# A second pair of blocks by seven products, a constant written later, and other banks for the second layer's first group

## The chip, the cores and the metric

The kernel runs on one core of one Trainium2 chip. The metric is device time in microseconds of one execution. Times in the trace are microseconds from the start of the profiled span unless marked ns.

The engines are named as the profile names them: PE is TensorE's matrix product and PEld its weight load, DVE is VectorE, ACT is ScalarE, POOL is GpSimd, SP is SyncE. A "product" below is one matmul instruction.

## The reference

A two-layer encoder over 512 tokens of width 1024. Each layer has a mixer of three gated attentions and then a feed-forward part with a convolution:

```python
def conv_ffn(h, w_up, conv_w, conv_b, w_down):
    u = h @ w_up                                  # 512 x 1024 by 1024 x 5632
    u = depthwise_conv_width_3(u, conv_w) + conv_b
    a, g = jnp.split(u, 2, axis=-1)               # 2816 each: "value" and "gate" half
    return (jax.nn.gelu(g) * a) @ w_down

for l in range(2):
    h = rmsnorm(x, norm1_g[l])
    x = x + gated_parallel_mixer(h, ...)          # three attentions, merged by gates, @ w_out
    h = rmsnorm(x, norm2_g[l])
    x = x + conv_ffn(h, ...)
return rmsnorm(x, final_g)
```

All data are float32. The up projection's 5632 columns are 44 blocks of 128: blocks 0 to 21 of the value half (p = 0) and 0 to 21 of the gate half (p = 1).

## The kernel before, in words

**Precision.** A float32 operand is split into a high part and the rest (`hi`, `lo`, both in the type fp32r), and each product of two operands is done as three: hi by hi, hi by lo, lo by hi (`mm3`, lines 222 to 224). Activations lie transposed, 128 features by 512 tokens, as eight tiles `hh`, `hl`; weights are the stationary side.

**A plain block.** `dense` multiplies one block of 128 output columns: 8 tiles of the inner dimension x 3 products, each 128 x 128 by 128 x 512, into one bank of PSUM (`ps_d`). Then `conv` (lines 1105 ff.) reads the bank: ScalarE writes `c` (L1113), VectorE adds the two neighbours (L1115, L1116). In a gate block ScalarE applies the GELU (L1120), VectorE multiplies with the value block kept in `ca` (L215 `prod`), and `operands` makes what the down projection reads: high and low parts of the product and of sums of its quarters (L1139 to L1155).

**Seven products.** Where two neighbouring blocks, pairs of inner tiles and the two halves of the tokens form a 2 x 2 x 2 product, the kernel uses seven half-size products instead of eight (a Strassen-like scheme). The down projection and part of the output projection do so for all columns (`do_sum`, L1175 to L1177). `do_us` does it for one pair of blocks of the up projection in each layer, chosen by `UPS = ((9, 1),)`: pair 9 of the gate half, blocks 18 and 19. A unit is 7 steps x 4 pairs of inner tiles x 3 products of 128 x 128 by 128 x 256 (L1066 to L1068), in four banks. It needs
- sums of weights: `load_sum` loads four quarters of the weight block (one of them twice) on SP's queue and adds two of them by adding DMAs from GpSimd's queue (lines 173, 174); VectorE makes two more sums (L189, L192);
- sums of the activations: `whole` copies `hh` to `hx` and adds `hl` by DMA, `mix` makes the sums and splits them (`hs`). This is done once a layer, after block 12, four times `mix` after four later blocks;
- evictions: partial results go to `u1`, `u2` by ScalarE (L1071 to L1081) and VectorE (L1075, L1079, L1084), and `conv` reads `u1`, `u2` instead of a bank.

**Order.** TensorE's and SP's instructions run in the order that `schedule` writes out by hand: value block and gate block in turn, `("up", f)`, the unit `("us", 9, 1)` in the place of its second block, then `cover`, `rest` and the sums of the down projection. VectorE's, ScalarE's and GpSimd's order in this part comes from a planner that knows priorities: splits of weights (300) and evictions (400) go ahead of the convolutions. Each engine runs its instructions in its order.

**Weights.** `fetch` loads weights into three `raw` tiles (sums also into `own` and `s` tiles) and splits them into three pairs `whi` (ScalarE, L208) and `wlo` (VectorE, L209). A pair becomes free when TensorE has finished the step three before.

**Banks.** `banks` names for each part of the kernel which of the eight PSUM banks each kind of use takes in turn; `bank` hands out the next of a group and waits, through its readers, until it is free. In the feed-forward part `d` is the ring 0, 1, 2, 3, 4, 5, 7, 6. `do_mla_open` starts a layer's mixer with a fixed list: `g` (the four banks of the first group, `do_lat`), `d`, and `r` (row sums). The second layer's first group follows directly on the first layer's last sum, whose last result is added to two tiles `x` by one VectorE instruction (L1185). Later, `do_mla_attn` names one ring for all, beginning with 7, 0, 1.

**The constant.** `eps`, one column of a small tile `cst`, is written by VectorE among the first instructions (line 94), right after two other constants of the same tile (lines 91, 92). It is read as a bias by ScalarE in the second norm of each layer (L495). TensorE begins with products on a tile of ones (`early`, `idle`, L432) that compute nothing, until the first operands are there.

Of the kernel before, what the change touches and what calls it, by code (L numbers as in the profile page):

```python
# [24 lines left out]
EPS = 1e-6  # L25
# [14 lines left out]
NP, AHEAD, EVAC = (6, 5, 4), (7, 4), 400  # L40
F2 = 2 * NP[0]
FIX = 6
UPS = ((9, 1),)
ORDERS = (("V11", "S1", "V12", "S2", "S4", "V22", "S3"), ("V11", "V12", "S1", "S2", "S4", "V22", "S3"))
B11, B21, B22, T1, T3, T2, T4 = range(7)
ROWS = (slice(0, 64), slice(64, 128))
# [19 lines left out]
class Trunk:  # L66
# [5 lines left out]
    def __init__(self, ctx, tc, d):  # L72
        self.tc, self.nc, self.d, self.ctx = tc, tc.nc, d, ctx
        nc = self.nc
        self.small = ctx.enter_context(tc.tile_pool(name="small", bufs=1))
        self.const = ctx.enter_context(tc.tile_pool(name="const", bufs=1))
        self.wp = ctx.enter_context(tc.tile_pool(name="wp", bufs=1))
        self.psum = ctx.enter_context(tc.tile_pool(name="psum", bufs=1, space=bass.MemoryType.PSUM))
        self.groups, self.turn = {}, {}
        c = self.const  # L80
        x0 = c.tile([P, S + NPC], F32, name="x0")
        self.x = [x0[:, :S]] + [c.tile([P, S], F32, name=f"x{k}") for k in range(1, KD)]
        self.par = [x0[:, S:], self.small.tile([P, NPC], F32, name="par1")]
        self.early = c.tile([P, P], F32, tag="acc", name="early")
        nc.vector.memset(self.early, 1.0)
        self.idf = c.tile([P, P], F32, name="idf")
        make_identity(nc, self.idf)
        self.mean = c.tile([P, P], F32R, name="mean")
        cst = self.small.tile([P, 7], F32, name="cst")
        self.neghalf, self.ones = cst[:, 0:4], cst[:, 4:5]  # L90
        nc.vector.memset(self.neghalf, -0.5)
        nc.vector.memset(self.ones, 1.0)
        self.eps = cst[:, 6:7]
        nc.vector.memset(self.eps, EPS)
        self.warm = cst[:, 5:6]
        nc.scalar.activation(self.warm, self.ones, AF.Exp)
        self.specs, self.raws, self.parts, self.used = [], {}, [], 0
        self.plans = [self.schedule(l) for l in range(L)]
        for s, W in self.plans:
            self.specs += [w for item in s for w in W.get(item, ())]  # L100
        nc.sync.dma_start(x0[:, :S + PC_CW], d["x0"])
        self.fetch(1, 0)
        for k in range(1, 5):
            nc.sync.dma_start(self.x[k], d["xT"][k * P:(k + 1) * P, :])
            self.fetch(min(k + 1, 3), 0)
        self.gmask = self.small.tile([P, 3 * P], BF16, name="gmask")
# [223 lines left out]
    def schedule(self, l):  # L330
# [30 lines left out]
        for f in ups[8:]:  # L361
            W["up", f] = [(d["w_up"][l], 0, KD, f * P, P)]
        for i, p in UPS:
            unit = {"w": d["w_up"][l], "m": p * NF + 2 * i, "part": 1, "np": 4, "r0": 0, "order": ORDERS[0]}
# [33 lines left out]
        seq[n - 8:n - 8] = [("sum", 0, m) for m in range(0, KD, 2)]  # L398
        for i, p in UPS:
            old = [("up", p * NF + 2 * i + e) for e in range(2)]  # L400
# [97 lines left out]


    def do_mla_open(self):  # L500
        self.banks(g=[0, 1, 2, 3], d=[4, 5, 0, 1, 2, 3], r=[6, 7])
        self.mxs, self.mx = self.open("mx")
        self.mps, self.mp = self.open("ml")
        self.mp2 = self.mps.enter_context(self.tc.tile_pool(name=f"mm{self.l}", bufs=1, reuse_waits="tile"))
        self.rc, self.rsn = (self.mp.tile([P, S], F32, tag=t, name="rope", bufs=2) for t in ("knh", "knl"))
        if self.l:
            self.rope_table()
        self.hb = self.small.tile([P, 24], F32, tag="hb", name="hb")
        self.nc.vector.tensor_scalar(self.hb, self.pr[:, PC_BG:PC_BG + 24], 0.5, None, ALU.mult)
        self.merged, self.z = [None] * KD, {}  # L510
        self.qn, self.kn, self.pts, self.pp, self.y = {}, {}, {}, {}, {}
# [27 lines left out]
    def do_lat4(self):  # L539
        if self.l == 0:  # L540
            rest = self.par[0][:, PC_CW:]
            for t, src in ((rest, self.d["par"][0][:, PC_CW:]), (self.par[1], self.d["par"][1])):
                self.nc.gpsimd.tensor_copy(t[:, 0:4], self.rt)
                self.nc.gpsimd.dma_start(t, src)
            self.nc.gpsimd.tensor_scalar(self.mean, self.idf, 0.0, 1.0 / D, ALU.mult, ALU.add)
        self.latent(4, self.dense(self.spec(), self.h))

# [609 lines left out]
    def do_sum(self, part, m):  # L1157
# [33 lines left out]
        elif m == KD - 2:  # L1191
# [3 lines left out]
            for _ in self.operands(F2):  # L1195
                pass
            if UPS:
                self.whole()
# [219 lines left out]
```

## Time and profile before

| | |
|---|---|
| median of 3 runs | 1665.04 us (1664.78 to 1665.18) |
| the profiled execution | 1664.89 us |
| its span, first to last instruction | 1663.1 us |
| TensorE busy | 1654.7 us, 99% of the span |
| VectorE busy | 1291.4 us, 78% |
| ScalarE busy | 948.3 us, 57% |
| GpSimd busy | 134.1 us, 8% |
| read from memory | 168.80 MB, 103 GB/s over the span |
| granted clock of TensorE | 1.000 |

The busy share is an average over stages with different limits. A product's duration in the trace is the life of a pipelined instruction: several overlap, so the time that a chain of products takes is read from the distance of their starts. A wait that the profile gives to an instruction is idle time of its engine just before it, with the instruction that released it.

In the first layer the unit of blocks 18 and 19 runs from 745.28 us, in the second from 1569.21 us; the second layer begins at 829.56 us.

### The profile page before, as it was taken

The page shows a single profiled execution, that of the slowest core. Times are in us where ns is not written, and L with a number is a line of the kernel's source. Part 1 is how long each engine was busy: PE and PEld are TensorE (multiplying, and loading weights), DVE is VectorE, ACT ScalarE, POOL GpSimd, SP SyncE. Part 2 cuts the span into 40 slices and gives each one's busy share as a digit, 9 for nine tenths or more (in the row PEclk, how much of TensorE's full clock was granted, in tenths as well). Part 3 has the DMA queues.
Part 4 walks back from the last instruction along what each step waited for, and adds up shares of the span by engine and source line. Part 5 has one row for each costly group of instructions (what it writes and reads, how often), then busy time and mean ns, then how long its engine had stood idle before and what let it go on. Part 6 is the DMA issues. An engine that isn't in the chain of part 4 may idle for free.

```text
span 1663.1 us, 25448 instructions
## 1 busy us (share of the span) xinstructions
PE 1654.7 (99%) x9480; PEld 1415.9 (85%) x9480; DVE 1291.4 (78%) x2256; ACT 948.3 (57%) x1704; POOL 134.1 (8%) x190
## 2 busy tenths in 40 slices
PE   9999999999999999999999999999999999999998
PEld 8888888888898889888987888888889888898888
DVE  7767866787889877797967677667878897777887
ACT  7664545775565544555566545467755655436554
POOL 2122100000000000100011220000001000001000
PEclk9999999999999999999999999999999999999999
DMA  6255523222534366636432564332236343657373
GB/s 183 74 125 114 139 84 95 77 77 74 140 97 133 101 149 155 153 96 165 110 105 80 112 146 106 98 89 77 64 85 150 90 127 101 164 131 175 96 168 94
DMA packets 326923, 191.22 MB, mean 115 GB/s; under 512 B 17072, under 2 KB 313792, under 8 KB 326800
## 3 DMA queue, kind: packets, MB, share of 16 engines
q1 hardware_dynamic: 304064, 162.38, 34.8%
q0 software_dynamic: 22448, 26.89, 9.6%
q8 instruction: 74, 1.21, 0.3%
q14 instruction: 49, 0.40, 0.1%
q10 hardware_dynamic: 288, 0.33, 0.1%
HBM read 168.80 MB, written 2.10 MB: 103 GB/s over the span
## 4 chain that ended last, share of the span: by engine, by line
PE 97%; DVE 1%; ACT 1%; issue 0%; DVEq 0%; ACTq 0%
PE ps_ring L222 13%; PE ps_ring L223 12%; PE ps_ring L224 12%; PE ps_d L222 9%; PE ps_d L224 9%; PE ps_d L223 9%; PE ps_d L1177 5%; PE ps_d L1176 5%; PE ps_d L1175 5%; PE ps_g L222 2%; PE ps_g L224 2%; PE ps_g L223 2%; PE ps_ring L303 2%; PE ps_ring L290 1%; PE ps_ring L792 1%; PE ps_g L323 1%
## 5 line engine op out<-in xcount | busy, mean ns | idle before, releaser
L208 ACT CAST whi<-raw 128x1024 fp32r<-128x1024 f32 (+5 forms) x353 | 291.3, 826 | 351.2 <-PE ps_ring L223 123.4
L209 DVE TENSOR_TENSOR wlo<-raw,whi 128x1024 fp32r<-128x1024 f32 (+5 forms) x351 | 331.4, 946 | 79.4 <-ACT whi L208 77.2
L222 PE MATMUL ps_ring<-hh,whi 128*128 128x512 f32 x600 | 235.6, 393 | 0.6 <-DVE pt L761 0.3
L224 PE MATMUL ps_ring<-hh,wlo 128*128 128x512 f32 x600 | 234.0, 390 | 0.0
L223 PE MATMUL ps_ring<-hl,whi 128*128 128x512 f32 x600 | 233.7, 390 | 0.0
L222 PE MATMUL ps_d<-hh,whi 128*128 128x512 f32 x589 | 229.4, 389 | 0.0
L223 PE MATMUL ps_d<-hl,whi 128*128 128x512 f32 x589 | 229.4, 389 | 0.0
L224 PE MATMUL ps_d<-hh,wlo 128*128 128x512 f32 x589 | 229.3, 389 | 0.0
L1176 PE MATMUL ps_d<-ft,whi 128*128 128x256 f32 x546 | 154.7, 283 | 0.0
L1177 PE MATMUL ps_d<-ft,wlo 128*128 128x256 f32 x546 | 154.7, 283 | 0.0
L1175 PE MATMUL ps_d<-ft,whi 128*128 128x256 f32 x546 | 154.7, 283 | 0.0
L222 PEld LDWEIGHTS ps_ring<-hh,whi 128*128 128x128 f32 x600 | 112.7, 188 | 24.8 <-DVE pt L761 0.6
L224 PEld LDWEIGHTS ps_ring<-hh,wlo 128*128 128x128 f32 x600 | 112.7, 188 | 23.7
L223 PEld LDWEIGHTS ps_ring<-hl,whi 128*128 128x128 f32 x600 | 112.7, 188 | 23.0
L224 PEld LDWEIGHTS ps_d<-hh,wlo 128*128 128x128 f32 x589 | 110.6, 188 | 23.1
L222 PEld LDWEIGHTS ps_d<-hh,whi 128*128 128x128 f32 x589 | 110.6, 188 | 22.7
L223 PEld LDWEIGHTS ps_d<-hl,whi 128*128 128x128 f32 x589 | 110.6, 188 | 22.7
L1176 PEld LDWEIGHTS ps_d<-ft,whi 128*128 128x128 f32 x546 | 104.9, 192 | 0.2
L1175 PEld LDWEIGHTS ps_d<-ft,whi 128*128 128x128 f32 x546 | 104.9, 192 | 0.2
L1177 PEld LDWEIGHTS ps_d<-ft,wlo 128*128 128x128 f32 x546 | 104.9, 192 | 0.0
L215 DVE TENSOR_TENSOR gz<-ps_ring,rb 128x512 f32<-128x512 f32 x44 | 30.4, 691 | 63.2 <-PE ps_ring L224 63.2
L222 PE MATMUL ps_g<-hh,whi 128*128 128x512 f32 x176 | 68.9, 391 | 0.9 <-DVE x L1185 0.9
(419 smaller groups left out, 3578.8 us busy)
## 6 DMA issues: line engine op xcount, KB each, us to landing
raw<-in_w_in_dram SPq DMA_DIRECT2D x86, 512.0 KB, 4.0
raw<-in_w_up_dram SPq DMA_DIRECT2D x68, 512.0 KB, 3.8
raw<-in_w_up_dram SPq DMA_DIRECT2D x36, 256.0 KB, 2.9
raw<-in_w_down_dram SPq DMA_DIRECT2D x18, 384.0 KB, 4.9
tm<-in_namask_dram SPq DMA_DIRECT2D x16, 384.0 KB, 4.3
tm<-in_rpb_dram POOLq DMA_DIRECT2D x48, 128.0 KB, 4.7
own<-in_w_down_dram SPq DMA_DIRECT2D x16, 384.0 KB, 5.9
raw<-in_w_in_dram SPq DMA_DIRECT2D x17, 256.0 KB, 3.2
```

The lines of the kernel that those rows point to most:

```text
L208: nc.scalar.copy(hi, src)
L209: nc.vector.tensor_sub(lo, src, r32(hi))
L215: self.nc.vector.tensor_tensor(out, a, b, ALU.mult)
L222: mm(ps, sh, mh, start=first and k == 0, stop=False)
L223: mm(ps, sh, ml, start=False, stop=False)
L224: mm(ps, sl, mh, start=False, stop=last and k == n - 1)
L290: self.nc.tensor.transpose(out[2 * u + i][:, c * 64:c * 64 + 64], block[q], self.idf[q, q])
L303: self.nc.tensor.matmul(out, st[a], mv[b], start=first and t == 0, stop=last and t == 2)
L323: self.nc.tensor.matmul(self.gbank[j], w[:, j * P:(j + 1) * P], m, start=n + t == 0, stop=False)
L1175: mm(ps, wh, hi, start=fresh and i == 0, stop=False, skip_group_check=True)
L1176: mm(ps, wh, lo, start=False, stop=False, skip_group_check=True)
L1177: mm(ps, wl, hi, start=False, stop=i == n - 1, skip_group_check=True)
```

## The change

Three edits:
1. `UPS` names a second pair: pair 8 of the gate half, blocks 16 and 17. `schedule` puts the unit `("us", 8, 1)` in the place of block 17's step and drops block 16's. TensorE's order around it was value 16, gate 16, value 17, gate 17, value 18, value 19, unit of 18 and 19; it becomes value 16, value 17, unit of 16 and 17, value 18, value 19, unit of 18 and 19. The sums of the activations are shared by both units.
2. `eps` is written by GpSimd in the first layer's `do_lat4`, not by VectorE at the start.
3. In the second layer `do_mla_open` takes its banks from the `d` ring of the layer before, in the order in which they were used: the four used longest ago for the first group. The first layer's list stays as it was.

```diff
-UPS = ((9, 1),)
+UPS = ((8, 1), (9, 1))
...
         self.eps = cst[:, 6:7]
-        nc.vector.memset(self.eps, EPS)
...
     def do_mla_open(self):
-        self.banks(g=[0, 1, 2, 3], d=[4, 5, 0, 1, 2, 3], r=[6, 7])
+        a = [0, 1, 2, 3, 7, 4, 5, 6]
+        if self.l:
+            a = [self.groups["d"][(self.turn["d"] + i) % 8] for i in range(8)]
+        self.banks(g=a[:4], d=[*a[5:7], *a[:4]], r=[a[7], a[4]])
...
                 self.nc.gpsimd.tensor_copy(t[:, 0:4], self.rt)
                 self.nc.gpsimd.dma_start(t, src)
+            self.nc.gpsimd.memset(self.eps, EPS)
             self.nc.gpsimd.tensor_scalar(self.mean, self.idf, 0.0, 1.0 / D, ALU.mult, ALU.add)
```

## Prediction

> **What bounds the kernel.** I read the page's shares first, then the chain that ended last, then TensorE's waits, and only then single stretches.
>
> ```profile
> PE 1654.7 (99%) x9480; PEld 1415.9 (85%) x9480; DVE 1291.4 (78%) x2256; ACT 948.3 (57%) x1704; POOL 134.1 (8%) x190
> PE 97%; DVE 1%; ACT 1%; issue 0%; DVEq 0%; ACTq 0%
> L222 PE MATMUL ps_d<-hh,whi 128*128 128x512 f32 x589 | 229.4, 389 | 0.0
> L1176 PE MATMUL ps_d<-ft,whi 128*128 128x256 f32 x546 | 154.7, 283 | 0.0
> ```
>
> TensorE is busy for 99% of the span and the chain that ended last is 97% TensorE, with no engine near it: VectorE stands at 78%. So time goes only where matmuls go, or where TensorE stops waiting. The last two rows are a warning: their means, 389 ns for 512 columns and 283 ns for 256, are lives of pipelined instructions. By them 84 products of 283 ns (23.8 us) would be dearer than 48 of 389 ns (18.7 us), and the change would lose 5 us a layer. What counts is the distance of their starts, below.
>
> All of TensorE's waits together are 3.4 us (us in total, times, longest):
>
> ```profile
> PE idle L432 <- DVE cst L92: 1.1, 1, 1.1
> PE ps_g L222 <- DVE x L1185: 0.9, 1, 0.9
> PE ps_ring L222 <- DVE pt L761: 0.6, 4, 0.2
> PE ps_ring L222 <- DVE nm L922: 0.6, 2, 0.3
> PE ps_a L1293 <- ACT o L1305: 0.2, 1, 0.2
> ```
>
> Two of them touch the change: 0.9 us on the `x` update of line 1185, and 1.1 us at the start on line 92, a write of the tile in which the moved constant lies.
>
> **The products.** The kernel already does one pair of blocks (18, 19 of the gate half) by seven products in each layer. It stands between two plain blocks, so one timeline of TensorE gives both prices (start, duration):
>
> ```profile
> 734.40 0.39 PE L222 MATMUL ps_d<-hh,whi 128*128 128x512 f32 x1
> ...
> 745.28 0.28 PE L1066 MATMUL ps_d<-hh,whi 128*128 128x256 f32 x1
> ...
> 755.23 0.28 PE L1068 MATMUL ps_d<-hs,wlo 128*128 128x256 f32 x1
> 755.35 0.40 PE L222 MATMUL ps_d<-hh,whi 128*128 128x512 f32 x1
> ```
>
> From 734.40 to 745.28 run two plain blocks, 2 x 8 x 3 = 48 products of 512 columns: 10.88 us, one each 0.2267 us. From 745.28 to 755.35 runs the pair by seven products: 7 x 4 x 3 = 84 products of 256 columns (28 from each of three lines, here one of them), 10.07 us, one each 0.1199 us.
>
> ```profile
> 745.00:756.00 11.00, 7.93 (x28) 1.00 0.33 96
> ```
>
> The second layer's unit says the same: 1579.28 - 1569.21 = 10.07 us.
>
> ```profile
> 1569.21 0.28 PE L1066 MATMUL ps_d<-hh,whi 128*128 128x256 f32 x1
> ...
> 1579.28 0.40 PE L222 MATMUL ps_d<-hh,whi 128*128 128x512 f32 x1
> ```
>
> So the new pair costs 10.88 - 10.07 = 0.81 us less in each layer. After such a unit the first plain products start slightly further apart; I take 0.03 us for that, leaving 0.78 us, or **1.56 us for two layers**. An ideal seven eighths would give 10.88 / 8 = 1.36 us a layer; the rest goes because 256 columns take 0.1199 us, not half of 0.2267 (0.1133): 84 x 0.0066 = 0.55 us.
>
> Here a rule of the Trainium skill would change the sum. "TensorE: Matmul & The Clock Gate", section "Back-to-back issue gap", puts the gap of starts at N / 2.4 ns plus 2.5 ns: 109 ns for 256 columns, 216 ns for 512. By it a unit would take 9.2 us against 10.4 us, an estimate of 1.2 us a layer, 0.8 us more over both layers than by the rows. The trace disagrees at both widths, 0.1199 and 0.2267 us, each about 11 ns above the rule, and the additional 36 products a layer pay that each time. I keep the rows.
>
> **The start of the second layer.** Columns: start, duration, and the wait before it.
>
> ```profile
> 828.41 0.28 PE L1177 MATMUL ps_d<-ft,wlo 128*128 128x256 f32 x1
> 829.56 0.47 PE L222 MATMUL ps_g<-hh,whi 128*128 128x512 f32 x1 [0.87 <-DVE x L1185]
> 829.87 0.40 PE L223 MATMUL ps_g<-hl,whi 128*128 128x512 f32 x1
> ```
>
> The last product of layer 1 starts at 828.41; the next would follow about 0.12 us later, but starts at 829.56. Its bank is the one that the last `x` update still reads. In a ring of eight, the old first layer takes 34 + 4 + 16 + 2 + 12 = 68 `d` banks before that point, so its last unit holds entries 0 to 3, and the fixed list begins with bank 0. After the change the count is 70, the last unit holds banks 2 to 5, and the new list begins at 7, 6, 0, 1. The gain is 829.56 - 828.41 - 0.12 = 1.03 us; the first two starts after the pause are 0.31 instead of 0.23 us apart, which may add 0.08. I take **1.0 us** (bounds 0.9 and 1.1). The fixed list would by now also begin on free banks (0, 1), so the seven products alone should remove this wait; the sum is the same.
>
> What is late next there? The new order makes later steps of this layer share banks differently. The first scores of the latent attention (line 303) take bank 1, which the gate block just before them used:
>
> ```profile
> 885.93 0.69 DVE L215 TENSOR_TENSOR ev<-ps_d,rbk 128x512 f32<-128x512 f32 x1 [3.88 <-POOL rbk L268]
> 887.91 0.68 DVE L215 TENSOR_TENSOR gz<-ps_d,rb 128x512 f32<-128x512 f32 x1
> ...
> 889.20 0.49 PE L303 MATMUL ps_ring<-kr,qr 64*128 64x512 f32 x1
> ```
>
> The gate's update ends at 887.91 + 0.68 = 888.59, and the scores start at 889.20: 0.6 us are left. The update is late because VectorE stands in order behind line 215 `ev`, which waited for the broadcast `rbk`. All of this chain starts from a transpose on TensorE, so it moves along with it: I take nothing, with a bound of +0.7 us, one such update.
>
> **What the pair adds elsewhere.** VectorE first: its splits of weights by shape, and single instructions of the old unit.
>
> ```profile
> L209 DVE TENSOR_TENSOR wlo<-raw,whi 128x1024 fp32r<-128x1024 f32 x158 | 193.0, 1223 | 50.2 <-ACT whi L208 49.5
> L209 DVE TENSOR_TENSOR wlo<-raw,whi 128x512 fp32r<-128x512 f32 x121 | 82.8, 687 | 18.1 <-ACT whi L208 16.8
> ...
> 742.01 0.69 DVE L189 TENSOR_TENSOR s<-s,own 128x512 f32<-128x512 f32 x1
> 749.79 0.42 DVE L1075 TENSOR_TENSOR u<-u,ps_d 128x256 f32<-128x256 f32 x1
> 756.57 0.68 DVE L1084 TENSOR_TENSOR u<-u,ps_d 128x512 f32<-128x512 f32 x1
> ```
>
> Added per layer: seven splits of 512 columns, 7 x 0.687 = 4.8 us; two sums of weights (lines 189 and, alike, 192), 2 x 0.69 = 1.4 us; three evictions, 2 x 0.42 (lines 1075 and, alike, 1079) + 0.68 = 1.5 us. Removed: two splits of 1024, 2.4 us. The net is **5.3 us more for VectorE**. None of it is on TensorE's path while VectorE can put off other work. Can it? Columns: stretch, its length, then busy us (and instructions) of TensorE, its loads, VectorE, ScalarE and GpSimd.
>
> ```profile
> 690.00:733.00 43.00, 43.00 (x191) 35.65 (x190) 41.38 (x64) 24.99 (x36) 1.72 (x2) 1.00 0.63 149
> 730.00:790.00 60.00, 60.00 (x306) 51.43 (x305) 46.94 (x71) 32.70 (x51) 3.44 (x4) 1.00 0.48 125
> 1515.00:1550.00 35.00, 35.00 (x156) 28.97 (x156) 34.14 (x55) 21.25 (x31) 1.43 (x2) 1.00 0.66 159
> 1550.00:1610.00 60.00, 60.00 (x309) 51.53 (x308) 49.96 (x75) 32.47 (x51) 3.73 (x5) 1.00 0.53 129
> ```
>
> From 690 to 733 VectorE is full: 41.4 of 43 us; it makes the sums that the seven products need, and TensorE doesn't stall in it. From 730 to 790 it has 60 - 46.9 = 13.1 us free, in the second layer 60 - 50.0 = 10.0 us. So 5.3 us fit in, but at 13.1 us free in 60 they take some 24 us: VectorE stays full through the new unit and into the old one. ScalarE is idle for over 40% of these stretches. What is urgent is weights and evictions: 7.7 us in the 10.1 us of a unit; convolutions can wait, as a plain block's bank comes round again only after eight. The nearest deadlines:
>
> ```profile
> 723.28 0.68 DVE L209 TENSOR_TENSOR hs<-tt,hs 128x512 fp32r<-128x512 f32 x1
> ...
> 751.64 0.37 ACT L1077 COPY u<-ps_d 128x256 f32<-128x256 f32 x1
> ...
> 753.63 1.23 DVE L209 TENSOR_TENSOR wlo<-raw,whi 128x1024 fp32r<-128x1024 f32 x1 [0.47 <-ACT whi L208]
> ```
>
> The new unit starts four plain blocks before 745.28, at 745.28 - 21.76 = 723.52. Its fourth product, at 727.8, is the first to read the last sums of operands, split at 723.28 to 723.97: 3.9 us to spare, less 0.85 us of added splits ahead of them. In the unit's bank 0, the copy at 751.64 ends at 752.01 and the seventh product writes there at 753.9: 1.9 us to spare. The first plain block behind the unit needs its low half in its third product, at 755.8, and has it at 753.63 + 1.23 = 754.86: 1.0 us. So the covers are 1.0 to 3 us thick, and VectorE's longest instruction is 1.2 us. I cost the pair's side work at nothing; without cover it is at most the 5.3 us a layer.
>
> DMA: two loads of 512 KB give way to five of 256 KB (SP's queue) and two adding transfers (GpSimd's).
>
> ```profile
> 717.16 0.57 SPq L170 DMA_DIRECT2D own<-in_w_up_dram  x1
> ...
> 723.02 0.86 POOL L173 DMA_DIRECT2D s<-own  x1 [33.24 <-DVE prod L215]
> ...
> 749.11 0.68 DVE L209 TENSOR_TENSOR wlo<-raw,whi 128x512 fp32r<-128x512 f32 x1
> ```
>
> For the old unit the loads start at 717.16 and the first adding transfer at 723.02, long before its second product at 746.7. The loads of the new unit stand early in the same way, and hold two of the three raw buffers meanwhile. The old unit's loads now queue behind block 19's, which needs the buffer that the new unit's fifth split frees: 749.11 + 0.68 - 745.28 = 4.5 us after its start, about 728. They are needed at 744.5 + 1.4 = 745.9, 18 us later; issue to adding transfer took 5.9 us, and its 0.86 us and landing follow. Nothing is late; cost nothing, at worst a few of these us.
>
> **The constant.** Columns as above.
>
> ```profile
> 0.97 0.06 DVE L94 MEMSET cst<- 128x1 f32 x1
> 4.08 0.22 DVE L155 CAST whi<-raw 128x128 fp32r<-128x128 f32 x1
> ...
> 4.41 0.66 PEld L323 LDWEIGHTS ps_g<-h,whi 128*128 128x128 f32 x2 [0.29 <-ACT h L467]
> ```
>
> The moved write is the last of three, 0.06 us long. TensorE's first wait, named after the one before it, ends in products that compute nothing; the first real weights are loaded at 4.41, after a cast that ends at 4.30 and had waited for data. So I take 0, at most 0.06 us. On GpSimd the write stands behind two copies and two loads of parameters, ahead of `mean`; its reader is some hundred us away.
>
> **Sum.** 1.56 + 1.0 + 0 = 2.6 us. The profiled execution took 1664.89 us (span 1663.1 and 1.8 around it), so 1662.3; the median of the runs is 0.15 us higher, so **1662.4 us**, 0.16% less. A measurement of this kernel tells about 0.2% (3.3 us) from no change; so the forecast itself is "within".
>
> **Rivals.**
> 1. *VectorE gives back part.* Behind the new unit a low half or a bank copy comes late by up to one VectorE instruction, 1.2 us a layer, in one or both layers. For it: covers of 1.0 us and a queue that stays full. Against: 43 us of full VectorE without a wait. Time 1662.4 + 0.5 to 2.4, say 1663.7.
> 2. *VectorE becomes the bound: slower.* Convolutions stand in its order ahead of the splits, so TensorE waits for the added work. It decides where the loss passes 1.3 us a layer; in full it is 1662.4 + 2 x 5.3 = 1673.0. Against it: 13.1 and 10.0 us free right behind.
> 3. *Narrow products cost half of wide ones.* Then 84 x 0.1133 = 9.52 us, a gain of 1.36 a layer, and the time is 1665.04 - 2.72 - 1.0 = 1661.3. Both units of the trace speak against it. The rule of the Trainium skill above lies between, at about 1661.6 (estimate).
> 4. *The start of the second layer gains nothing*, because another wait (the gate's bank, +0.7 us) takes its place: 1662.4 + 0.7 to 1.0, about 1663.3.
>
> **How the numbers follow.** The forecast 0.60 (own range 1661.9 to 1662.9), rival 1 0.18, rival 2 0.12, rival 3 0.04, rival 4 0.06. The range 1661.6 to 1664.8 takes in the forecast, rivals 1 and 4 and leaves out rivals 2 and 3. Faster by over 0.2%, below 1661.7, is rival 3 and the edge of the forecast: 0.06. Slower by over 0.2%, above 1668.4, is the larger half of rival 2: 0.07. Within: 0.87.
>
> **What the profile after would show.** Two timelines with a start of the first narrow product and of the plain one after the unit 10.07 us apart, twice a layer; TensorE's list of waits without line 1185 and with none at lines 1066 to 1068; the first product of the second layer's group 0.12 us after the last of the first; VectorE near 10 of 10 until about 755 and 1580; the scores at line 303 without a wait. I am wrong if TensorE waits for `wlo`, `whi` or `hs` between 723 and 760, or in the same place of the second layer, or if the order of VectorE elsewhere changes so that the attention stages wait more than their 1.2 us.

## The result and the profile after

The changed kernel takes 1673.59 us (median of 4 runs, 1672.52 to 1675.24) against 1665.10 (1664.78 to 1665.18): ratio 1.0052, 95% interval 1.0035 to 1.0070. It is slower by 8.5 us; the forecast was 1662.4. The profiled execution took 1673.58 us, span 1671.8.

TensorE's list of waits after (us in total, times, longest) has lost line 1185 and gained the first row below (two more rows, of 0.3 and 0.2 us, are new too); the lines after are numbered a little differently (the products of these units stand at 1069 to 1071, the low splits at 208, the convolution's taps at 1118 and 1119):

```profile
PE ps_d L1071 <- DVE wlo L208: 6.6, 6, 1.9
PE idle L431 <- DVE cst L92: 1.1, 1, 1.1
```

The first layer's new unit, the plain pair behind it and its old unit, then the second layer's two units, each stretch bounded by the start of a unit's first product and of the first product behind it. Columns: stretch, its length, busy us (and instructions) of TensorE, its loads, VectorE, ScalarE, GpSimd, then granted clock, DMA share, GB/s:

```profile
723.62:735.50 11.88, 10.84 (x86) 10.27 (x84) 11.01 (x19) 7.10 (x13) 0.00 (x0) 1.00 0.26 74
735.50:746.41 10.91, 10.91 (x51) 9.01 (x50) 7.21 (x11) 5.36 (x9) 1.72 (x2) 1.00 0.82 185
746.41:759.18 12.77, 10.68 (x85) 10.21 (x84) 12.53 (x22) 9.00 (x17) 0.00 (x0) 1.00 0.22 62
1550.24:1562.14 11.90, 10.85 (x86) 10.28 (x84) 11.02 (x19) 6.86 (x12) 0.00 (x0) 1.00 0.27 76
1573.05:1587.81 14.76, 12.18 (x86) 11.73 (x84) 13.13 (x23) 9.41 (x17) 0.00 (x0) 0.88 0.25 72
```

A unit took 10.07 us before. After, the four take 11.88, 12.77, 11.90 and 14.76, together 11.0 us more than 4 x 10.07. The plain pairs that they replace gave 2 x 0.81 back, and the start of the second layer 1.02 (its first product now comes 0.12 us after the last one of the layer before):

```profile
832.25 0.28 PE L1180 MATMUL ps_d<-ft,wlo 128*128 128x256 f32 x1
832.37 0.40 PE L221 MATMUL ps_g<-hh,whi 128*128 128x512 f32 x1
```

-1.62 - 1.02 + 11.03 is +8.4; the rest of the span's +8.7 is 0.3 us ahead of the first of these units and behind the last. So everything that was forecast as a gain came, and the loss lies in four stretches of 10 us. In each, TensorE stops before the third product of a group of three, the one that reads the low half `wlo` (start, duration, wait):

```profile
730.08 0.28 PE L1070 MATMUL ps_d<-hl,whi 128*128 128x256 f32 x1
731.34 0.39 PE L1071 MATMUL ps_d<-hh,wlo 128*128 128x256 f32 x1 [0.98 <-DVE wlo L208]
...
751.38 0.28 PE L1070 MATMUL ps_d<-hs,whi 128*128 128x256 f32 x1
753.58 0.39 PE L1071 MATMUL ps_d<-hs,wlo 128*128 128x256 f32 x1 [1.93 <-DVE wlo L208]
```

VectorE is busy for 11.0 of 11.9 and 12.5 of 12.8 us of these stretches. In all four units it is idle for 0.03 us at most from the unit's start to the last of its stalls; the rest of its idle time comes behind that. Its order in front of the second of the stalls:

```profile
749.71 0.42 DVE L1153 SCALAR_TENSOR_TENSOR tt<-tt,prod 128x256 f32<-128x256 f32 x1
750.05 0.68 DVE L1152 TENSOR_TENSOR ft<-prod,ft 128x512 fp32r<-128x512 f32 x1
750.65 0.68 DVE L191 TENSOR_TENSOR raw<-s,raw 128x512 f32<-128x512 f32 x1
751.25 0.41 DVE L1154 SCALAR_TENSOR_TENSOR tt<-tt,prod 128x256 f32<-128x256 f32 x1
751.59 0.74 DVE L1118 SCALAR_TENSOR_TENSOR c<-ps_d,x,c 128x511 f32<-128x511 f32 x1
752.25 0.68 DVE L1156 TENSOR_TENSOR ft<-tt,ft 128x512 fp32r<-128x512 f32 x1
752.85 0.68 DVE L208 TENSOR_TENSOR wlo<-s,whi 128x512 fp32r<-128x512 f32 x1
```

The split `wlo<-s` that TensorE waits for from 751.65 runs at 752.85. Right ahead of it stand two subtractions and two steps of the down projection's operands (lines 1152 to 1156), a tap of a convolution (one of its two outer terms, 1118) and a weight sum (191). Of these TensorE needs only the sum within this unit. The stretch before the unit shows how the backlog came about: VectorE sat idle for 2.1 us, because the split in its order read data of an adding transfer that were not there yet (queues of SyncE and GpSimd, then ScalarE and VectorE).

```profile
711.67 20.01 SPq L139 DMA_DIRECT2D raw<-in_w_up_dram  x2
731.73 0.58 SPq L169 DMA_DIRECT2D own<-in_w_up_dram  x1
...
737.59 0.86 POOL L172 DMA_DIRECT2D s<-own  x1 [30.59 <-DMA s<-in_w_up_dram]
...
743.93 0.62 ACT L207 CAST whi<-s 128x512 fp32r<-128x512 f32 x1 [2.27 <-issue]
...
741.69 0.75 DVE L1118 SCALAR_TENSOR_TENSOR c<-u,x,c 128x511 f32<-128x511 f32 x1
744.59 0.69 DVE L208 TENSOR_TENSOR wlo<-s,whi 128x512 fp32r<-128x512 f32 x1 [2.14 <-ACT whi L207]
```

SyncE's queue spent 20.0 us on two loads, 19.2 of them waiting for a split on VectorE to free a raw buffer, so the second unit's loads start at 731.73; the adding transfer on GpSimd follows at 737.59 and lands 6.3 us later, and ScalarE casts its data at 743.93. That is in time for TensorE (second group of the unit, from 746.41 + 1.44 = 747.85), but VectorE reached the split at 742.4 and does nothing else meanwhile.

One more thing costs time in the second layer only. Behind the last stall the clock drops:

```profile
1573.05:1580.70 7.65, 5.07 (x40) 4.62 (x38) 7.62 (x15) 5.69 (x11) 0.00 (x0) 1.00 0.00 0
1580.70:1584.20 3.50, 3.50 (x19) 3.50 (x20) 3.34 (x6) 0.89 (x2) 0.00 (x0) 0.61 0.49 142
1584.20:1587.81 3.61, 3.61 (x30) 3.61 (x29) 2.17 (x3) 2.84 (x4) 0.00 (x0) 0.90 0.53 157
```

Products that follow each other at 0.12 us elsewhere stand 0.21 us apart from 1581.54 to 1584.74. With 0.90 granted to the unit's end this makes about 1.5 of the 2.0 us by which that unit is longer than the first layer's; its stalls are 0.5 us longer. Of the 11.0 us over all four units the waits are 6.6 and the clock 1.5; the other 2.9, 0.7 a unit, lie in starts further apart: 0.22 in place of 0.12 us right before and behind a stall (1578.27 to 1578.49, 1580.70 to 1580.92), and 0.34 us between two products where the list shows no wait (726.61 to 726.95).

### The profile page after: what moved, and what is told of

It reads as the page before. It is cut to its first block, busy times and chain, and to the rows that moved or that the text cites. A ratio compares the mean times of both kernels' runs of the same rounds, so it can differ in the third digit from the quotient of the medians.

```text
span 1671.8 us, 25673 instructions
## 1 busy us (share of the span) xinstructions
PE 1656.8 (99%) x9552; PEld 1418.9 (85%) x9552; DVE 1298.8 (78%) x2275; ACT 953.7 (57%) x1722; POOL 138.2 (8%) x195
## 3 DMA queue, kind: packets, MB, share of 16 engines
q8 instruction: 75, 1.23, 0.3%
## 4 chain that ended last, share of the span: by engine, by line
PE 89%; DVE 3%; DMA 2%; ACT 2%; issue 2%; POOL 0%; SPq 0%; DVEq 0%; ACTq 0%; POOLq 0%
PE ps_ring L221 12%; PE ps_ring L222 12%; PE ps_ring L223 12%; PE ps_d L223 8%; PE ps_d L222 8%; PE ps_d L221 8%; PE ps_d L1180 5%; PE ps_d L1179 5%; PE ps_d L1178 5%; PE ps_g L223 2%; PE ps_g L221 2%; PE ps_g L222 2%; PE ps_ring L302 2%; PE ps_ring L289 1%; PE ps_ring L795 1%
## 5 line engine op out<-in xcount | busy, mean ns | idle before, releaser
L207 ACT CAST whi<-raw 128x1024 fp32r<-128x1024 f32 (+4 forms) x355 | 290.8, 820 | 352.5 <-PE ps_ring L222 123.3
L208 DVE TENSOR_TENSOR wlo<-raw,whi 128x1024 fp32r<-128x1024 f32 (+4 forms) x353 | 330.4, 938 | 79.0 <-ACT whi L207 77.0
L221 PE MATMUL ps_d<-hh,whi 128*128 128x512 f32 x557 | 216.8, 389 | 0.0
L222 PE MATMUL ps_d<-hl,whi 128*128 128x512 f32 x557 | 216.7, 389 | 0.0
L223 PE MATMUL ps_d<-hh,wlo 128*128 128x512 f32 x557 | 216.7, 389 | 0.0
L223 PEld LDWEIGHTS ps_d<-hh,wlo 128*128 128x128 f32 x557 | 104.6, 188 | 21.7
L222 PEld LDWEIGHTS ps_d<-hl,whi 128*128 128x128 f32 x557 | 104.6, 188 | 21.5
L221 PEld LDWEIGHTS ps_d<-hh,whi 128*128 128x128 f32 x557 | 104.6, 188 | 21.5
L223 PE MATMUL ps_g<-hh,wlo 128*128 128x512 f32 x176 | 68.7, 391 | 0.1
```

Of the source, the lines that this page charges most:

```text
L207: nc.scalar.copy(hi, src)
L208: nc.vector.tensor_sub(lo, src, r32(hi))
L221: mm(ps, sh, mh, start=first and k == 0, stop=False)
L222: mm(ps, sh, ml, start=False, stop=False)
L223: mm(ps, sl, mh, start=False, stop=last and k == n - 1)
```

## The experiments

The theories at the start. **1**: VectorE works in order, and inside a unit more stands in front of the urgent splits than fits (the second rival of the prediction). **2**: the second unit's loads and adding transfers come too late. **3**: neither, but the chain of a unit itself (split, weight sum, cast, split through three buffers). Times below are medians, the ratios are to the kernel before on the same chip.

**Which part of the change.** Only the second pair was added to the kernel before:

```
-UPS = ((9, 1),)
+UPS = ((8, 1), (9, 1))
```

> The kernel before with nothing but the second pair by seven products; the constant and the bank order are the old ones. Theory 1 (VectorE full and in order): all of the loss is the pair's, so 1673.6 us as the whole change gives, the unit at 16 and 17 at 11.9 us and the one at 18 and 19 at 12.8 and 14.8 us for 84 products each, against 10.07. The wait at the start of the second layer goes here too, if the turn of the bank ring (two more banks taken per layer) does it alone, as the prediction said; if only the new bank order takes it away, 1674.6. A rival that puts part of the loss on the bank order or the constant expects less than 1672.

1673.12 us, ratio 1.0046 (1.0033 to 1.0059). The whole loss is the pair's. The second layer starts 37.79 us after the first layer's first seven-product unit of the down projection (37.80 in the changed kernel, 38.82 before): the two more banks that the pair takes from the ring are enough to take the wait away, and the constant and the new bank order add nothing that shows.

The other way round, the change without the pair (`UPS = ((9, 1),)` in the changed kernel):

> The changed kernel with the second pair of blocks taken back (only blocks 18 and 19 by seven products); the constant and the bank order stay changed. All theories: no unit at blocks 16 and 17, so none of its stalls; what is left is the bank order, which takes away the 1.0 us wait of the second layer's first group on the bank read for `x` (profile of before), and the constant, which should be nothing. Expected 1664.1 us against 1665.1 before (0.9994). If the wait at the layer's start only moves to another reader, 1665.1.

1665.52 us, ratio 1.0000 (0.9992 to 1.0009). The layer starts 1.0 us earlier, but the gain is gone at 886 us: the first product of the attention's bank ring now waits for a reader of its bank:

```profile
PE ps_ring L221 <- DVE ev L214: 1.0, 1, 1.0
...
886.08 0.47 PE L221 MATMUL ps_ring<-mg,whi 128*128 128x512 f32 x1 [1.03 <-DVE ev L214]
```

**Taking VectorE's work away.** The changed kernel without the outer taps of the gate half's blocks 16 to 19:

```
+        if not 16 <= fi - NF < 20:
             nc.vector.scalar_tensor_tensor(c[:, 1:], u[:, :S - 1], cw[:, 0:1], ...)
             nc.vector.scalar_tensor_tensor(c[:, :S - 1], u[:, 1:], cw[:, 2:3], ...)
```

> The changed kernel, but the gate half's blocks 16 to 19 leave out the two outer taps of their convolution, 8 VectorE instructions of about 0.66 us a layer, 5.3 us: as much VectorE work as the new pair adds, taken out at the place of the stalls; loads, adding DMAs, splits and products are untouched. The output of those blocks is therefore that of a one-tap convolution. Theory 1 (VectorE is full there, and the taps and operand work stand ahead of the splits): the stalls go, units at 10.1 to 10.6 us each, total about 1662.5, at most 1665. Rival 2 (the second unit's loads and adding DMAs come too late): only the first unit's 2 x 1.8 us go, the second unit's 2.7 and 4.7 us stay, about 1669.9. Rival 3 (not the amount but the chain split, sum, cast, split through three split buffers): the stalls stay within 1 us of what they are, above 1671.

1669.66 us, ratio 1.0024 (1.0015 to 1.0034): just what theory 2 expected. But the trace shows that the taps were taken out in the wrong place. The first units stay at 12.1 and 11.7 us and the second fall to 11.5 and 11.9, since the taps inside a unit's stretch are those of the two value blocks before it. So the same again with `if not 16 <= fi < 20:`, the value half:

> The changed kernel, but the value half's blocks 16 to 19 leave out the two outer taps of their convolution, 8 VectorE instructions of 0.66 us a layer. The run that left out the gate half's taps of these blocks freed little inside the units: the trace shows that the taps which stand between a unit's splits are those of the two value blocks just before it. Here these are gone, 4 (2.6 us) out of each unit's stretch; everything else is as in the changed kernel. Theory 1 (VectorE's in-order work ahead of the splits): the stalls of 1.8, 2.7, 1.8 and 4.7 us go nearly all, units at 10.1 to 10.6 us, total 1662.5 to 1664.5. Rival 2 (second unit's loads late): 1669.9. Rival 3 (the chain split, sum, cast, split through three split buffers): above 1671.

1664.14 us, ratio 0.9992 (0.9984 to 1.0001). Its four units, columns as above:

```profile
724.07:734.14 10.07, 10.07 (x85) 10.07 (x84) 8.55 (x15) 7.89 (x14) 0.00 (x0) 1.00 0.41 115
745.05:755.55 10.50, 10.32 (x86) 10.12 (x85) 9.54 (x17) 8.27 (x15) 0.00 (x0) 1.00 0.26 71
1546.63:1556.83 10.20, 10.20 (x86) 10.13 (x85) 8.82 (x15) 7.06 (x13) 0.00 (x0) 1.00 0.40 109
1567.73:1578.41 10.68, 10.32 (x85) 10.11 (x84) 9.71 (x17) 8.11 (x15) 0.00 (x0) 1.00 0.25 69
```

The four units are at 10.07, 10.50, 10.20 and 10.68 us, with VectorE at 8.6 to 9.7 us in them. And the transfers are nearly as late as in the changed kernel: the first adding transfer is issued 9.7 us before the second unit's start, against 8.8 us. VectorE waits for them as long, and TensorE hardly notices (GpSimd's queue, VectorE, TensorE):

```profile
735.38 0.86 POOL L172 DMA_DIRECT2D s<-own  x1 [27.65 <-DMA s<-in_w_up_dram]
...
742.38 0.69 DVE L208 TENSOR_TENSOR wlo<-s,whi 128x512 fp32r<-128x512 f32 x1 [2.08 <-ACT whi L207]
...
748.50 0.39 PE L1071 MATMUL ps_d<-hh,wlo 128*128 128x256 f32 x1 [0.18 <-DVE wlo L208]
```

This is against theories 2 and 3 as sole causes, and it corrects what the run before it seemed to say. One thing besides the taps differs: with them gone the planner orders VectorE's other instructions anew. The second unit's split of `s` follows the split before it directly (747.76, 748.36), where in the changed kernel five others stand between them beside a tap. So this run shows that room on VectorE takes the stalls away, and leaves open how much of it is the amount of work and how much the order.

**Moving the late loads.** Only the second unit's five loads go to another queue; the order on VectorE and ScalarE is the changed kernel's:

```
-            self.nc.sync.dma_start(unit[name]...
+            (self.nc.gpsimd if (part, unit["np"], unit["m"]) == (1, 4, NF + 18) else self.nc.sync).dma_start(unit[name]...
```

> The changed kernel with the five loads of the unit at 18 and 19 issued by GpSimd's queue in place of SyncE's, so that they no longer wait behind block 19's load (18 us before they are used in the changed kernel's trace); VectorE's and ScalarE's instructions stand in the same order as in the changed kernel, nothing left out. Theory 1: the order decides, the weight sum of that unit starts no earlier in VectorE's row; its 2.7 and 4.7 us stay to within 1 us each, total 1671.5 to 1674. Rival 2 (late loads and adding DMAs): the second unit falls to 10.1 us, total 1673.6 - 7.4 = 1666.2.

1668.60 us, ratio 1.0019 (1.0010 to 1.0029): 5.0 us of the loss gone, where theory 1 expected at most 2. The adding transfer is at 708 in place of 737, and VectorE does the split of `s` at 742.36 (744.59 before this edit) without idling:

```profile
708.12 1.80 POOL L172 DMA_DIRECT2D s<-own  x2 [9.68 <-DMA s<-in_w_up_dram]
...
741.69 0.75 DVE L1118 SCALAR_TENSOR_TENSOR c<-u,x,c 128x511 f32<-128x511 f32 x1
742.36 0.68 DVE L208 TENSOR_TENSOR wlo<-s,whi 128x512 fp32r<-128x512 f32 x1
```

The second units fall from 12.77 and 14.76 to 10.74 and 11.89 us, the latter with the lower clock gone too (1.00 over the unit); the first stay at 12.01 and 11.57. So theory 2 holds for the second unit, in a form that I had not put down: the late transfer doesn't stop TensorE, it stops VectorE, and VectorE has no time left in the unit to make it good.

**Moving VectorE's work to GpSimd.** First 11 subtractions a layer of the operands:

```
+        eng = nc.gpsimd if 13 <= f < 18 else nc.vector
-        nc.vector.tensor_sub(at(lo, T1, 2), a, r32(at(hi, T1, 2)))
+        eng.tensor_sub(at(lo, T1, 2), a, r32(at(hi, T1, 2)))
...
```

> The changed kernel with the low-part subtractions of the down projection's operands for blocks 13 to 17 on GpSimd in place of VectorE: 11 instructions of about 0.6 us a layer, 6.6 us off VectorE at the place of the stalls, nothing left out. Theory 1: the splits come earlier, the units fall to 10.1 to 11 us, total 1662.5 to 1666. Rival 2 (late transfers): the second unit keeps its 2.7 and 4.7 us, 1669.9 or more, since GpSimd now also stands ahead of the adding DMAs. Rival 3 (the chain through three split buffers): 1671 or more.

1702.48 us, ratio 1.0222 (1.0208 to 1.0236): a failed relief, 29 us slower than the changed kernel. GpSimd's row and VectorE's at the first unit:

```profile
714.62 1.25 POOL L1157 TENSOR_TENSOR ft<-tt,ft 128x512 fp32r<-128x512 f32 x1
715.82 1.03 POOL L173 DMA_DIRECT2D raw<-own  x1
...
715.90 0.69 DVE L1047 TENSOR_TENSOR tt<-hx 128x512 f32<-128x512 f32 x1 [11.43 <-POOL ft L1157]
716.51 2.75 DVE L208 TENSOR_TENSOR wlo<-raw,whi 128x1024 fp32r<-128x1024 f32 x1
```

A subtraction takes 1.25 to 1.8 us there (0.68 on VectorE); the adding transfer of line 173 now stands behind them in GpSimd's order, 10 us later; VectorE waits 11.4 us for a buffer that GpSimd still reads, and a split of 1024 columns beside a GpSimd subtraction takes 2.75 us in place of 1.23. It says nothing on the theories, since it brings waits of its own.

Then only the two weight sums of each unit, which stand behind GpSimd's adding transfers anyway:

```
-            self.nc.vector.tensor_add(unit["S4"], unit["S2"], unit["V12"])
+            (self.nc.gpsimd if (unit["part"], unit["np"]) == (1, 4) else self.nc.vector).tensor_add(unit["S4"], ...
```

> The changed kernel with the two weight sums of each seven-product unit of the up projection on GpSimd in place of VectorE: 2 instructions of 0.6 us per unit off VectorE, on GpSimd some 1.3 to 1.5 us each (what the operand subtractions took there). Nothing left out. Theory 1: up to 1.2 us of each unit's stall goes, 1673.6 - 4 x 1.2 = 1668.8, if VectorE isn't slowed by GpSimd's instructions beside it. Rival 3 (the chain split, sum, cast, split decides): each chain grows by about 0.8 us, total 1675 or more. Rival 2: about 1673.6, no change.

1669.95 us, ratio 1.0029 (1.0017 to 1.0040): 3.6 us better, near theory 1's 4.8 and against theory 3, as the chain grew and the units shrank (11.20, 12.42, 11.34, 13.08 us). Here too the planner moves some of VectorE's other instructions. Both reliefs together, the loads and the sums:

> The changed kernel with both reliefs that helped: the second unit's five loads on GpSimd's queue (1668.6 us alone) and the weight sums of both units on GpSimd (1670.0 alone). Nothing left out. If the two take away different stalls (theory: late loads stall VectorE in front of the unit, full VectorE holds up the splits inside it), the gains add: 1673.6 - 5.0 - 3.6 = 1665.0. If both only buy the same slack, about 1667 to 1668. Below 1664 if the rest of the stalls goes too, since a shorter backlog frees VectorE also in the first unit.

1666.70 us, ratio 1.0007 (0.9998 to 1.0016): of 8.6 us expected 6.9 came. The units are 11.17, 10.27, 11.17 and 11.24 us, still 3.6 us over, and the change is now no longer slower than can be measured, but gains nothing.

**Moving the pair.** Units at blocks 16, 17 and 20, 21 (`UPS = ((8, 1), (10, 1))`):

> The changed kernel with the second unit at blocks 20 and 21 in place of 18 and 19: 22 us of plain blocks between the units in place of 11. Theory 1: the unit at 16 and 17 stays at 11.9 us (+1.8 a layer), that at 20 and 21 meets a VectorE that had 1.9 to 2.6 us free there before and comes at 10.1 to 11 us: total 1665.1 - 1.6 + 3.6 + 0 to 2 = 1667.1 to 1669.1 (1 us less if the second layer starts earlier). Rival 2 (late loads): the unit's loads come as late as before relative to it, and it keeps 2.7 and 4.7 us: 1673.6. Rival 3 (the chain of a unit by itself): every unit stalls the same, also where VectorE has time, 1.8 us each: 1670.7.

1671.63 us, ratio 1.0039 (1.0026 to 1.0051): above theory 1's 1667.1 to 1669.1 and below theory 2's 1673.6. Theory 3's 1670.7 is nearest, but it had every unit stall alike. The profiled execution, 1674.25 us, is the longest of its runs. The units at 20, 21 run without a stall (10.07 and 10.08 us), those at 16, 17 stall by themselves (11.61 and 12.12), so the first unit's loss doesn't need a neighbour. But now the down projection, which comes next, waits for VectorE (TensorE's waits):

```profile
PE ps_d L1071 <- DVE wlo L208: 2.2, 3, 1.0
PE ps_d L1180 <- DVE wlo L208: 1.3, 2, 0.9
PE ps_d L1179 <- DVE ft L1158: 1.2, 1, 1.2
```

At 18, 19 and 20, 21 (`UPS = ((9, 1), (10, 1))`), where VectorE had the most room:

> The changed kernel with the second unit at blocks 20 and 21 and the first at 18 and 19, none at 16 and 17, where VectorE was full before (10.89 of 11.0 us). VectorE had 2.2 + 0.75 + 1.9 us free from 745 to 777 us in the kernel before. Theory 1 (only the amount): 5.3 us into these, 0.4 to 1.5 us lost a layer: 1665.1 - 1.6 - 1.0 + 0.8 to 3 = 1663.3 to 1665.5. With the late loads of a second unit 11 us behind the first one (4.9 us in the changed kernel): 1668 to 1671. If the backlog moves into the down projection's operands, as with units at 16 and 20, 2.6 us more than the first of these: 1666 to 1668.

1668.65 us, ratio 1.0019 (1.0010 to 1.0028). The units are nearly clean (10.08, 10.73, 10.07, 10.72 us), and the backlog comes back in the down projection, mostly in the second layer. TensorE's list has the last two rows above again, with the same 1.3 and 1.2 us; the stretch:

```profile
1608.93:1620.00 11.07, 8.65 (x67) 8.04 (x66) 10.21 (x19) 7.22 (x11) 1.72 (x2) 1.00 0.70 153
```

From 1608.93 to 1620.00 TensorE is busy 8.7 of 11.1 us, VectorE 10.2. With both reliefs at this place as well:

> The changed kernel with its units at 18, 19 and 20, 21, the weight sums of both on GpSimd and the loads of the second on GpSimd's queue; nothing left out. Units there alone gave 1668.7: the units stood only 0.7 us late a layer, but VectorE's backlog came back in the down projection, 0.7 us in the first layer and 3.2 us in the second. Theory 1: the sums take 2.4 us a layer off VectorE, the early loads another 2 us of its waiting, and the backlog is about gone: 1662.5 to 1665.0. If GpSimd's instructions slow VectorE's own beside them or hold up the adding DMAs, 1666 to 1668.

1668.96 us, ratio 1.0022 (1.0012 to 1.0031), a miss: all four units take 10.07 us, but the second layer's down projection still waits:

```profile
PE ps_d L1179 <- DVE ft L1152: 1.3, 1, 1.3
PE ps_d L1178 <- ACT ft L1146: 0.9, 1, 0.9
```

Both are operands of the last blocks. The reliefs emptied the units and not that place. The trace shows late loads again, now those of the down projection's weights (ScalarE, VectorE):

```profile
1605.91 0.73 ACT L207 CAST whi<-own 128x640 fp32r<-128x640 f32 x1 [4.20 <-DMA own<-in_w_down_dram]
...
1606.67 0.83 DVE L208 TENSOR_TENSOR wlo<-own,whi 128x640 fp32r<-128x640 f32 x1 [2.99 <-ACT whi L207]
```

SyncE's queue issues the loads of the first seven-product unit there from 1597.58 us on (1583.43 in the kernel before), a cast waits 4.2 us for one of them, and VectorE behind it is idle for 3.0 us, 6 us before TensorE's first wait there. That this makes the waits is argued; no run moved those loads. In this execution, 1670.72 us and 1.8 above the median, the clock also fell behind the two waits, to 0.62 from 1616.50 to 1621.00, which is about 1.7 us.

**Adding VectorE's work alone.** Was it the amount, 5.3 us a layer? The kernel before, with no second pair, and the taps of value blocks 16 to 19 applied twice:

```
+        for _ in range(2 if 16 <= fi < 20 else 1):
             nc.vector.scalar_tensor_tensor(c[:, 1:], u[:, :S - 1], cw[:, 0:1], ...)
             nc.vector.scalar_tensor_tensor(c[:, :S - 1], u[:, 1:], cw[:, 2:3], ...)
```

> The kernel before, without the second pair, but the value half's blocks 16 to 19 apply the two outer taps of their convolution twice: 8 more VectorE instructions of 0.66 us a layer, 5.3 us, the amount that the pair adds, with no load, adding DMA, split or product changed. The output of those blocks is therefore that of other taps. Theory 1 (VectorE's amount of work and its order): 18 and 19 at 11 to 12.5 us in place of 10.07, and some of it later in the down projection, together 2 to 6 us: 1667 to 1671. Rival 2 (late loads alone): no loads are later, so 1665.1 within 0.5. Rival 3 (the chain of the unit): no change either.

1665.44 us, ratio 1.0000 (0.9991 to 1.0008): that amount costs nothing here, against theory 1 as it stood. Three times the taps (`range(3 ...`):

> The kernel before, without the second pair, but the value half's blocks 16 to 19 apply the two outer taps of their convolution three times: 16 more VectorE instructions of 0.66 us a layer, 10.6 us; the output of those blocks is that of other taps. With them twice VectorE was busy 10.4 of 11.3 us before the unit and 9.6 of 10.1 us in it, and nothing was lost. Theory 1, as it now stands (a unit stalls once VectorE's work inside its stretch is more than the products' 10.07 us): 11.5 to 12.5 us of work fall into the stretch, the unit comes at 11 to 12.5 us, and what VectorE is late by is lost once more in the down projection: 1665.2 + 2 to 7 = 1667 to 1672. Rival: full VectorE alone stalls nothing, it takes the weight sums, the late loads or the chain of a second unit: 1665.2 to 1666.

1670.06 us, ratio 1.0027 (1.0016 to 1.0039). The two units with twice the taps:

```profile
745.11:755.18 10.07, 10.07 (x85) 10.07 (x84) 9.80 (x16) 5.95 (x11) 0.00 (x0) 1.00 0.24 68
1569.09:1579.37 10.28, 10.28 (x85) 10.16 (x84) 10.04 (x17) 5.81 (x11) 0.00 (x0) 1.00 0.24 67
```

and with three times the taps, with one of TensorE's waits in it:

```profile
745.33:757.68 12.35, 10.70 (x85) 10.23 (x84) 12.35 (x22) 6.40 (x12) 0.00 (x0) 1.00 0.20 56
1571.67:1583.70 12.03, 10.39 (x86) 10.18 (x84) 12.03 (x21) 6.34 (x12) 0.00 (x0) 1.00 0.20 56
...
753.51 0.39 PE L1068 MATMUL ps_d<-hh,wlo 128*128 128x256 f32 x1 [1.64 <-DVE wlo L209]
```

With 9.8 and 10.0 us of VectorE work in the unit it takes 10.07 and 10.28 us; with 12.35 and 12.03 it takes as long as VectorE, with loads, sums and transfers as in the kernel before. The wait is again one for a low half, 1.64 us. The two units are 4.2 us longer together, nearly the whole loss of 4.4; the further loss in the down projection that theory 1 expected didn't come.

**A version that beats both.** The change without the pair, with the bank ring of the second layer started one bank later:

```
-        self.banks(ring=[7, 0, 1, 2, 3, 4, 5, 6])
+        self.banks(ring=[0, 1, 2, 3, 4, 5, 6, 7] if self.l else [7, 0, 1, 2, 3, 4, 5, 6])
```

> The changed kernel without the second pair, and with the bank ring of the second layer's attention starting at bank 0 in place of bank 7. In the run without the second pair the layer's start came 1.0 us earlier, but at 886.1 us the first product of that ring waited 1.03 us for VectorE's reading of the same bank (one product group before). If that wait is all that gave the gain back, it goes here and the time is 1665.5 - 1.0 to 1.4 = 1664.1 to 1664.5. If another reader of the shifted ring takes its place, 1665.5 again.

1663.98 us, ratio 0.9992 (0.9983 to 1.0000): the wait for `ev` is gone from TensorE's list, and 1.2 us are kept. It is the fastest of all kernels here, by less than one such comparison can tell for sure.

## Why the prediction was wrong

**The products: right.** A plain pair against the old kind of unit was 0.81 us a layer in the trace before, and a unit without a wait is 10.07 us nearly everywhere (blocks 16, 17 without the value taps; blocks 20, 21), 10.20 to 10.28 us at three places. So the rows were the better guide than the rule of the Trainium skill that the prediction set beside them ("TensorE: Matmul & The Clock Gate", "Back-to-back issue gap"), by which such a unit would take 9.2 us (estimate). That section gives the rule for a product by itself, and says that it is too low for narrow and too high for wide products in a stream with weight loads; at 512 columns the trace, 226.7 against 216 ns, has it too low as well.

**The start of the second layer: right**, 1.0 forecast and 1.02 measured, and also that the pair alone removes this wait. That a wait of the same size appears further on where the ring isn't shifted (886 us, without the pair) was my rival 4 in kind, but at line 221 and not at 303, and only in the kernel without the pair.

**The constant: right**, as far as 1673.59 against 1673.12 us, from two comparisons, can tell.

**The step that failed** is "I cost the pair's side work at nothing", and with it the sentence on the transfers, "Nothing is late; cost nothing". It was worth +11.0 us. The prediction's own sign of being wrong is there, TensorE waiting for `wlo` between 723 and 760 us. Rival 2 came true in kind, TensorE waiting for splits behind other work of VectorE, and I had given it 0.12. That its price fits so well, 1673.0 forecast and 1673.6 measured, is luck: it was the whole added work of 5.3 us a layer, which alone costs nothing (taps twice), and the measured loss holds late loads and a lower clock that the rival didn't have. The mistakes, as the runs show them:
- *The room was counted over the wrong length.* I read 13.1 us free in a stretch of 60 us and called 5.3 us hidden. What counts is the 10 us of one unit. Leaving out the run with GpSimd's subtractions, units with VectorE busy for 10.1 us or less take 10.07 to 10.73 us, those with 10.2 to 13.6 take 10.7 to 14.9. (A stalled unit is longer and so holds more work; the runs with taps taken out and added show which way the cause goes.) I had the number for it in hand (7.7 us of urgent work in 10.1), and set it aside with "convolutions can wait". TensorE doesn't need them soon, but they and the operands' steps stand in VectorE's order where the program put them, ahead of the splits.
- *The thickness of the cover was taken from three deadlines* (the operands of the fourth product, the seventh product's bank and the first plain block behind the unit: 3.9, 1.9 and 1.0 us), where no stall came. The stalls came at the unit's own weights: the four long ones (0.98, 1.93, 0.98, 1.93 us) at a weight sum's low half, the two short ones (0.17, 0.65) at that of a plain quarter. In a plain block a split of 1024 columns feeds 24 products, 5.4 us; in a unit a split of 512 feeds 12, 1.44 us. The same three buffers of splits are 16 us of products ahead there and 4.3 us here.
- *"Against: 43 us of full VectorE without a wait"* argued from plain blocks, whose splits are that much earlier.
- *The loads were 18 us early for TensorE only.* They came at 731.7, not 728, and to the landing of the adding transfer it took another 12 us. The reader that counts is the split's place in VectorE's order, 742.4, and there the data were 2.1 us late. The move of the loads gave 5.0 us back.
- *Not in any rival*: the lower clock behind two stalls close together, about 1.5 us of the 11.0.

How the 11.0 us divide: 5.0 go with the second unit's late loads alone (the clock's 1.5 among them), 3.6 with the weight sums off VectorE alone, 6.9 with both, 9.5 without the value half's taps. These are not parts of a sum: as I read them, each buys the same thing, room for VectorE inside a unit. Shown is that TensorE waits for a VectorE without idle time, that taking work off it or starting its loads earlier takes stalls away, that enough added work makes one (taps three times, where the unit takes as long as VectorE), and that 5.3 us a layer by themselves are harmless where they can spread. Not shown is how much is VectorE's amount of work and how much its order: of these runs only the one with the earlier loads kept the order, and one with the splits ahead of the operands' steps, all else the same, wasn't tried.

## What to carry to other kernels

Compare a side engine's work with the length of the stretch in which it is urgent, not with its idle share over the layer: here 5.3 us more were free when they left VectorE under some 10 us in the 10 us of a unit, and the pair's 5.3 us, with its late loads, cost 11 us. When a block is cut into shorter products, the same ring of buffers is ahead by less time, so look for the engine whose lead shrinks. A transfer has to be in time for the place of its reader in an in-order engine's queue, not for the final consumer.

## What the runs showed of the hardware

- After two stalls within 5 us (0.65 and 1.93 us without a product, 1576 to 1580.7) the granted clock was 0.61 over the next 3.5 us, and starts of products went from 0.12 to 0.21 us apart. After a stall of 1.93 us with one of 0.17 before it (749 to 753.6), or of 1.64 us alone in the run with three-fold taps, no such drop is seen. Two stalls alone don't settle it either: behind 0.95 and 1.16 us (1621.06 and 1623.79 us, units at 16 and 20) the clock was 0.57 over 4 us, behind 0.94 and 1.17 us (1616.23 and 1618.97, units at 18 and 20) it stayed at 1.00. What decides is open. The Trainium skill ("TensorE: Matmul & The Clock Gate", "What's actually happening") knows a full and a half rate, the lower one after an idle window of some 3.4 us. The half rate agrees: the trace has 0.50 from 1582 to 1584 us, and 0.21 in place of 0.12 us. The idle window, taken as one pause, doesn't, as the longest without a start was 2.2 us.
- GpSimd's subtraction of 512 columns took 1.25 to 1.8 us, and a split of 1024 columns on VectorE beside one of them 2.75 us in place of 1.23 (twice, once a layer). The Trainium skill ("SBUF — State Buffer", "SBUF: two separate sides") says that a VectorE instruction with two inputs in SBUF and a GpSimd one that reads SBUF share a pair of ports, which the one that starts first holds for the whole instruction while the other is blocked. An additional 1.52 us beside a GpSimd instruction of 1.55 us fits the block; by the profile, though, the split had started 0.1 us earlier, so who came first isn't shown.
- From the issue of an adding transfer (737.59) to the cast that reads it (743.93) passed 6.3 us; I had counted 0.86 us and a landing without a number. The first unit's two adding transfers, issued at 704.40 and 706.13, landed after 3.3 and 3.9 us.
